# Moving the weight halves by 128 bytes in SBUF: two pad tiles of a two-layer hybrid-attention kernel resized

## The chip, the cores and the metric

The kernel runs on one NeuronCore of a Trainium2 chip. The metric is the device time of one execution in microseconds (us). TensorE multiplies matrices (the profile calls its matmuls PE and its weight loads PEld), VectorE is DVE, ScalarE is ACT, SyncE is SP and issues the transfers. SBUF is the on-chip memory: 128 partitions, and a tile takes the same byte range in each of them. What is changed here is where in that byte range the tiles stand.

## What is computed

Two layers act on one sequence of 256 tokens of width 1024, all in float32. A layer is a token mixer (sparse attention A with a top-64 selection, low-rank attention B, two gated branches, an output projection), a layer norm, a convolutional feed-forward network of inner width 2816, and a second layer norm. Shifts, scales and gates come from a conditioning vector `c`.

```python
def reference(x, c, ...):
    for l in range(DEPTH):                                   # DEPTH = 2
        mod = jax.nn.silu(c) @ w_ada[l] + b_ada[l]
        sh1, sc1, g1, sh2, sc2, g2 = jnp.split(mod[:, None, :], 6, axis=-1)
        h = x * (1.0 + sc1) + sh1
        y = token_mixer(h, positions, rel_bias, w_in[l], ...)
        x = layer_norm(DEEPNORM_ALPHA * x + g1 * y, ln1_g[l], ln1_b[l])
        h = x * (1.0 + sc2) + sh2
        y = conv_ffn(h, w_up[l], conv_w[l], conv_b[l], w_down[l])
        x = layer_norm(DEEPNORM_ALPHA * x + g2 * y, ln2_g[l], ln2_b[l])
    return x
```

## The kernel before

Activations stand with features on the partitions and the 256 tokens along the free dimension. All weights come as one long stream from HBM, in units of up to 2048 columns. `load` (from L192) issues each unit on the queue of SP into one of four `raw` tiles, as soon as the unit that had the tile is done with.

A float32 product is made of three faster ones. ACT rounds 1024 columns of a unit to the type float32r (`hi`, L245), DVE subtracts to get the rest (`lo`, L246); four tiles of each take turns. Activations are split in the same way into a tile with `hh` in its name and one with `hl` (`hhm`, `hlm` for the mixer, `hhf`, `hlf` for the feed-forward network, `h2h`, `h2l` for its inner activations, `nh`, `nl`, `ybh` and so on for smaller ones). `mm3` (L288) then issues hi·hh, hi·hl and lo·hh for each block of 128 output features: the weight block of 128 x 128 is loaded into TensorE as the stationary operand, 512 bytes a partition, and the activations are streamed past it as the moving operand, 256 columns or 1024 bytes a partition. Each matmul has its own weight load, so the two read SBUF at the same time, all through a stage. One stage has the roles the other way round: `main_va` (L610) loads blocks of `hhm` and `hlm` and streams `hi` and `lo`.

In the order of the program a layer is: `g1` (six banks of the input projection at once), `qa` and `va` with the index scores (`sc`, L549) between their matmuls, `uq`, `uk`, `uv`, the gates `ga` and `gb` with the attention's matmuls between them, the branches `wb` and `wa`, the output projection `wo`, then the feed-forward network: `up` (8 blocks together), 18 units `upp0` to `upp17` and the down projection `dn`. With 8 input blocks, 8 + 36 output blocks of `up` and `upp` and 22 x 8 of `dn`, and three passes each, that is 192 + 18 x 48 + 528 = 1584 matmuls a layer. In the names of the trace a digit for the layer and some buffer numbers are left in: `upp00b` is unit 0 of layer 0, `upp171b` unit 17 of layer 1, `b` the bank.

The places in SBUF follow from the order in which three pools are opened (`cp` for what lives throughout, `wp` for what streams through, `ap_` for activations) and from the sizes of the tiles. Two tiles that nothing uses, `wpad` and `apad` (L154, L155), move what comes behind them: `wpad` is the first tile of `wp`, `apad` of `ap_`.

Of the kernel before, what the change touches and what calls it, by code (L numbers as in the profile page):

```python
# [9 lines left out]
F32 = mybir.dt.float32  # L10
# [7 lines left out]
P = 128  # L18
# [121 lines left out]
def _build(nc, tc, ctx, stream, xt, cbc, ctr, posl, vecs, cst, outp, dbg=None):  # L140
    cp = ctx.enter_context(tc.tile_pool(name="cp", bufs=1))
    wp = ctx.enter_context(tc.tile_pool(name="wp", bufs=1))
    ap_ = ctx.enter_context(tc.tile_pool(name="ap", bufs=1))
# [7 lines left out]
        return pp.tile([P, 512], F32, name=name, tag=tag, bufs={"mm": 3, "at": 4, "st": 1}[tag])  # L151


    wp.tile([P, 24], F32, name="wpad", tag="wpad", bufs=1)  # L154
    ap_.tile([P, 232], F32, name="apad", tag="apad")  # L155


    pos_i = wp.tile([P, 64 + T], I32, name="pos_i", tag="cv", bufs=4)
# [992 lines left out]
```

## Time and profile before

| | |
|---|---|
| median of 3 runs | 818.27 us (816.04, 818.27, 823.65) |
| the profiled execution | 814.9 us, of which 813.1 us is the span that the trace covers |
| TensorE: matmuls, weight loads | busy 97% and 93% of the span, 6708 of each |
| VectorE, ScalarE | busy 84% and 63% |
| granted TensorE clock | 0.998 in the mean |
| transfers | 182 MB, 224 GB/s in the mean |

The profiled execution is 3.4 us under the median and 1.1 us under the fastest of the three runs. The span runs from the first to the last instruction; the 1.8 us beside it lie around it. Matmuls overlap in the pipeline, so the length that the trace gives for one (about 280 ns) is not what one costs: that is read from the distance of the starts, or from the chain of waits, which adds up what each stretch of matmuls took.

### The profile page before, as it was taken

To read this page: it belongs to the slowest core of one execution; us is meant where nothing else is said; L and a number is where in the kernel's file an instruction comes from. 1 tells how busy PE (TensorE), PEld (TensorE's weight loads), DVE (VectorE), ACT (ScalarE), POOL (GpSimd) and SP (SyncE) were. 2 spreads that over 40 slices of the span, in tenths; PEclk is the share of its full clock that TensorE was granted. 3 is DMA by queue.
4 is the path that set the end of the run, shared out by engine and by line. 5 is a ranking of instruction groups with operands and counts; after the bars stand their busy time and mean duration, and the time that the engine had idled before them with its cause. 6 is when DMAs were issued, how large, how long until landed. Compare 5 with 4: busy or idle time off the path is not lost.

```text
span 813.1 us, 16736 instructions
## 1 busy us (share of the span) xinstructions
PE 787.8 (97%) x6708; PEld 759.6 (93%) x6708; DVE 683.3 (84%) x1377; ACT 514.1 (63%) x898; POOL 0.2 (0%) x4
## 2 busy tenths in 40 slices
PE   5999999999999999999999998999999999999996
PEld 4898899989999999999999998998999999999995
DVE  6878798989997998899888898766899799897674
ACT  5987566564578766653547856647447976765452
POOL 0000000000000000000000000000000000000000
PEclk9999999999999999999999999999999999999999
DMA  8885758778655575579777856745564555565621
GB/s 295 319 327 204 233 176 310 292 268 304 223 192 183 183 256 166 184 260 328 294 253 240 295 178 233 260 174 189 216 206 163 203 199 194 184 242 195 213 73 52
DMA packets 29727, 182.07 MB, mean 224 GB/s; under 512 B 3857, under 2 KB 5841, under 8 KB 10578
## 3 DMA queue, kind: packets, MB, share of 16 engines
q1 hardware_dynamic: 29650, 181.01, 63.0%
q8 instruction: 52, 0.85, 0.4%
q14 instruction: 25, 0.20, 0.1%
HBM read 178.84 MB, written 1.05 MB: 221 GB/s over the span
## 4 chain that ended last, share of the span: by engine, by line
PE 73%; DVE 14%; DMA 5%; ACT 5%; issue 2%; SPq 0%; ACTq 0%; DVEq 0%
PE dn L290 15%; PE up L290 6%; DVE lo L246 5%; DMA raw<-stream 5%; DVE raw L231 2%; ACT hi L245 2%; PE wo L290 1%; PE g L290 1%; ACT step L378 1%; DMA pr<-misc 1%; PE adap L262 1%; PE bl L656 1%; PE gb11b L290 1%; PE gb10b L290 1%; PE qa00b L290 1%
## 5 line engine op out<-in xcount | busy, mean ns | idle before, releaser
L245 ACT ACTIVATE hi<-raw 128x1024 fp32r<-128x1024 f32 (+3 forms) x255 | 254.8, 1004 | 194.8 <-PE dn L290 48.1
L246 DVE TENSOR_TENSOR lo<-raw,hi 128x1024 fp32r<-128x1024 f32 (+3 forms) x255 | 293.1, 1154 | 73.8 <-ACT hi L245 72.6
L231 DVE SCALAR_TENSOR_TENSOR raw<-raw,cb 128x1024 f32<-128x1024 f32 x90 | 107.5, 1219 | 12.4 <-DMA raw<-stream 7.1
L290 PE MATMUL dn<-h2h,lo 128*128 128x256 f32 x352 | 98.3, 279 | 0.0
L290 PE MATMUL dn<-h2l,hi 128*128 128x256 f32 x352 | 98.3, 279 | 0.0
L290 PE MATMUL dn<-h2h,hi 128*128 128x256 f32 x352 | 98.1, 279 | 0.0
L290 PEld LDWEIGHTS dn<-h2h,lo 128*128 128x128 f32 x352 | 66.9, 190 | 0.1
L290 PEld LDWEIGHTS dn<-h2l,hi 128*128 128x128 f32 x352 | 66.1, 188 | 0.0
L290 PEld LDWEIGHTS dn<-h2h,hi 128*128 128x128 f32 x352 | 66.1, 188 | 0.0
L290 PE MATMUL g<-hhm,hi 128*128 128x256 f32 x168 | 45.6, 291 | 5.1 <-ACT hhm L1020 5.0
L290 PE MATMUL g<-hhm,lo 128*128 128x256 f32 x168 | 44.5, 286 | 0.0
L290 PE MATMUL g<-hlm,hi 128*128 128x256 f32 x168 | 42.5, 280 | 0.0
L290 PEld LDWEIGHTS g<-hhm,hi 128*128 128x128 f32 x168 | 32.0, 195 | 7.3 <-ACT hhm L1020 6.8
L675 ACT ACTIVATE pr<-pr,mx 128x128 f32<-128x128 f32 x64 | 28.4, 446 | 12.3 <-DVE mx L672 12.3
L290 PE MATMUL up<-hhf,lo 128*128 128x256 f32 x128 | 34.8, 279 | 0.0
L290 PE MATMUL up<-hhf,hi 128*128 128x256 f32 x128 | 34.6, 280 | 0.0
L290 PE MATMUL up<-hlf,hi 128*128 128x256 f32 x128 | 33.2, 280 | 0.0
L290 PEld LDWEIGHTS g<-hhm,lo 128*128 128x128 f32 x168 | 31.8, 196 | 0.2 <-DVE lo L246 0.2
L290 PEld LDWEIGHTS g<-hlm,hi 128*128 128x128 f32 x168 | 30.3, 188 | 0.1
L290 PEld LDWEIGHTS up<-hhf,lo 128*128 128x128 f32 x128 | 24.3, 190 | 0.0
L290 PEld LDWEIGHTS up<-hhf,hi 128*128 128x128 f32 x128 | 23.8, 188 | 0.5 <-DVE hhf L973 0.5
L378 ACT ACTIVATE step<-posf,thr 128x256 bf16<-128x256 f32 (+1 forms) x64 | 23.2, 443 | 1.4 <-DVE thr L346 1.4
(904 smaller groups left out, 2665.5 us busy)
## 6 DMA issues: line engine op xcount, KB each, us to landing
raw<-stream SPq DMA_DIRECT2D x149, 1024.0 KB, 4.9
raw<-stream SPq DMA_DIRECT2D x21, 768.0 KB, 4.9
raw<-stream SPq DMA_DIRECT2D x5, 512.0 KB, 4.4
raw<-stream SPq DMA_DIRECT2D x4, 384.0 KB, 3.5
kT<-rl SPq DMA_DIRECT2D x8, 128.0 KB, 4.3
XB<-xt SPq DMA_DIRECT2D x3, 256.0 KB, 8.1
out<-XA SPq DMA_DIRECT2D x3, 256.0 KB, 2.5
XB<-xt SPq DMA_DIRECT2D x2, 128.0 KB, 6.4
```

The source lines that it names most:

```text
L231: V.scalar_tensor_tensor(out=raw[:, c:c + D], in0=raw[:, c:c + D], scalar=1.0, in1=cb, op0=OP.mult, op1=OP.mult, accum_out=mod[l][:, j:j + 1])
L245: S.activation(hi[:, a:e], raw[:, c + a:c + e], AF.Copy)
L246: x = V.tensor_sub(lo[:, a:e], raw[:, c + a:c + e], hi[:, a:e].bitcast(F32))
L262: PE.matmul(b[:, :T], ct[:, k:k + 1].to_broadcast([P, P]), raw[:, k * T:(k + 1) * T], start=(k == 0), stop=(k == KD - 1))
L290: PE.matmul(out, whl[p // 2][:, wcol], xhl[p % 2][xsl], start=start and p == 0, stop=stop and p == 2, skip_group_check=True)
L378: S.activation(st, posf[:, 64 + (0 if g < 32 else P):], AF.Sign, bias=thr[:, g:g + 1])
L656: PE.matmul(bs[e][:, P:384], q[:, P:T], k, start=False, stop=True, skip_group_check=True)
L675: S.activation(p[:, sl], p[:, sl], AF.Exp, bias=mx[:, j:j + 1], scale=-1.0, accum_out=ssum[:, h, j:j + 1])
```

## The change

`wpad` grows from 24 to 56 columns, 128 bytes, and `apad` shrinks from 232 to 200, the same 128 bytes. So all of `wp` moves up by 128 bytes, and the rest stays. The order of the instructions on each engine, and what each one works on, is the same row by row.

```diff
-    wp.tile([P, 24], F32, name="wpad", tag="wpad", bufs=1)
-    ap_.tile([P, 232], F32, name="apad", tag="apad")
+    wp.tile([P, 56], F32, name="wpad", tag="wpad", bufs=1)
+    ap_.tile([P, 200], F32, name="apad", tag="apad")
```

The byte at which the tiles start in a partition, modulo 256, as the built programs have it:

| tiles | before | after |
|---|---|---|
| `hi`, `lo` (all 8 tiles; every weight block in them is a multiple of 512 bytes further) | 0 | 128 |
| `raw`, `cv`, `pr`, `rl`, `rsA`, `mt` (the few small tiles of `wp` move by the same 128) | 0 | 128 |
| `hh..`, `hl..`, `h2h`, `h2l`, `nh`, `nl`, `ybh`, `yah`, `gate` and all else of `ap_` | 192 | 192 |
| `XA`, `XB`, `cb` (of `cp`) | 0 | 0 |
| the part of `vec` that is loaded with 470 columns | 64 | 64 |

For the pair of addresses that TensorE reads at once, moving minus stationary modulo 256, this gives:

| stage | before | after |
|---|---|---|
| all stages through `mm3` (weights stationary) | 192 - 0 = 192 | 192 - 128 = 64 |
| `va` (activations stationary) | 0 - 192 = 64 | 128 - 192 = 192 |

## Rows read from the trace of the kernel before

**Rows 1.** The page: busy time of each engine, share of the span, instructions.

```profile
PE 787.8 (97%) x6708; PEld 759.6 (93%) x6708; DVE 683.3 (84%) x1377; ACT 514.1 (63%) x898; POOL 0.2 (0%) x4
```

**Rows 2.** The page: chain that ended last, shares of the span by engine.

```profile
PE 73%; DVE 14%; DMA 5%; ACT 5%; issue 2%; SPq 0%; ACTq 0%; DVEq 0%
```

**Rows 3.** The same chain in order of time, layer 0: start us, us, what, matmuls.

```profile
105.85 5.65 PE ga00b L290 x48
...
213.34 5.44 PE wo20b L290 x48
...
230.26 22.73 PE up L290 x192
253.00 5.65 PE upp00b L290 x48
...
349.11 5.65 PE upp170b L290 x48
...
372.88 44.65 PE dn L290 x379
```

**Rows 4.** The same chain, layer 1, and one of its transfers.

```profile
440.39 7.37 DMA raw<-stream
...
496.82 5.47 PE ga01b L290 x48
...
620.33 22.12 PE up L290 x192
642.45 5.44 PE upp01b L290 x48
...
734.93 5.44 PE upp171b L290 x48
...
757.41 43.65 PE dn L290 x385
```

**Rows 5.** Windows, TensorE alone: stretch, us, busy (x), granted clock, DMA share, GB/s.

```profile
253.00:355.00 102.00, 102.00 (x868) 1.00 0.57 196
642.40:745.00 102.60, 102.60 (x908) 1.00 0.58 203
```

**Rows 6.** Timeline, layer 1, qa behind sc: start us, length, engine, line, out<-moving,stationary.

```profile
466.57 0.39 PE L290 MATMUL qa11b<-hhm,hi 128*128 128x256 f32 x1
466.79 0.28 PE L290 MATMUL qa11b<-hlm,hi 128*128 128x256 f32 x1
...
467.14 0.28 PE L290 MATMUL qa11b<-hlm,hi 128*128 128x256 f32 x1
...
469.18 0.28 PE L290 MATMUL qa11b<-hlm,hi 128*128 128x256 f32 x1
```

**Rows 7.** The same timeline, layer 1, va behind sc.

```profile
474.14 0.39 PE L610 MATMUL va<-hi,hhm 128*128 128x256 f32 x1
474.37 0.28 PE L610 MATMUL va<-lo,hhm 128*128 128x256 f32 x1
...
474.60 0.28 PE L610 MATMUL va<-hi,hhm 128*128 128x256 f32 x1
...
484.02 0.28 PE L610 MATMUL va<-hi,hlm 128*128 128x256 f32 x1
```

**Rows 8.** Groups by line and shape: busy us, mean ns, idle before.

```profile
L246 DVE TENSOR_TENSOR lo<-raw,hi 128x512 fp32r<-128x512 f32 x16 | 11.0, 688 | 1.3 <-ACT hi L245 1.1
L764 DVE TENSOR_TENSOR hlg<-gate,hhg 128x512 fp32r<-128x512 f32 x8 | 5.2, 688 | 0.0
...
L824 ACT ACTIVATE h2h<-sq 128x256 fp32r<-128x256 f32 x44 | 17.8, 405 | 4.5 <-DVE sq L822 4.4
L1027 ACT ACTIVATE XA<-XB 128x256 f32<-128x256 f32 x8 | 2.8, 406 | 1.3 <-DMA XB<-xt 1.3
```

**Rows 9.** Transfers: out<-in, count, KB of one, us from issue to landing.

```profile
raw<-stream SPq DMA_DIRECT2D x1, 256.0 KB, 5.6
...
vec<-vecs SPq DMA_DIRECT2D x1, 235.0 KB, 5.0
```

## The prediction, made before the changed kernel was run

> **What bounds the kernel now.** I read the page first, for the engine that is busy, then the chain of waits in order of time, for what a matmul costs in each stage, then the timeline around pauses, and last the groups and transfers for what else touches the moved tiles. TensorE is busy 97% of the span, and its weight loads 93% [rows 1]: a load runs beside nearly every matmul. Of the chain that ended last, 73% is TensorE, 14% VectorE and 5% transfers [rows 2]. So the kernel is bound by the pace of its matmuls, above all in the two feed-forward networks, where the chain is TensorE without a break.
>
> That pace has two values. In layer 0 a unit of 48 matmuls of `upp` takes 5.65 us, the first as the last of 18, which is 117.7 ns a matmul; in layer 1 the same unit takes 5.44 us, 113.3 ns, again from the first to the last [rows 3, 4]. `up` takes 22.73 us and 22.12 us for 192 matmuls. A part of `dn` takes 44.65 us for 379 in layer 0, 117.8 ns, and 43.65 us for 385 in layer 1, 113.4 ns. The granted clock is 1.00 in both layers, over 102 us each, and so are the transfers much alike, a share of 0.57 and 0.58 [rows 5]; neither makes the difference. I call the two paces fast (113.3) and slow (117.8); the step between them is 4.4 ns a matmul.
>
> It is not the places alone either. `wo` and `upp` of layer 0 read the same `hi`, `lo` and `hh` tiles in the same way, and `wo20b` takes 5.44 us for its 48 where `upp00b` takes 5.65 [rows 3]. The gate `ga`, with the same tiles in both layers, takes 5.65 us in layer 0 and 5.47 in layer 1 [rows 3, 4]. So with weights at 0 and streams at 192 both paces exist, and a stretch keeps the one in which it has settled: 18 units of `upp` in a row.
>
> What a stretch settles at behind a pause is where the place shows. In layer 1 `qa` and `va` are interrupted by the same index scores. Behind them `qa` starts at 466.57 us, the second matmul follows after 0.22 us, and from 467.14 to 469.18 us there are 18 steps, 113.3 ns each: fast [rows 6]. `va` starts at 474.14 us, the second matmul follows after 0.23 us, and from 474.60 to 484.02 us there are 80 steps, 117.8 ns each: slow [rows 7]. `va` has the roles exchanged: its moving operand minus its stationary one is 64 modulo 256, where it is 192 in `qa`. That 64 is what the change gives to every stage but `va`.
>
> **The change part by part.** It removes and adds no instruction, and no wait; order and queues are the same. Four things read or write what moves.
>
> First, TensorE. If the pair's difference decides where a stretch settles, all stages through `mm3` now settle as `va` did, slow. The change in time is then counted in matmuls on the chain that were fast before, by 4.4 ns each. The feed-forward network of layer 1 has 1584 of them: 1584 x 4.44 ns = 7.0 us. Checked against the rows: `up` 22.73 - 22.12 = 0.6 us, 18 x (5.65 - 5.44) = 3.8 us, and 528 x 4.4 ns = 2.3 us for `dn`, together 6.7 us; I take 7.0. `ga` of layer 1 has three whole units at the fast pace, 3 x 0.18 = 0.5 us, and the last three units of `wo` have 144 matmuls in each layer, 288 x 4.44 ns = 1.3 us [rows 3, 4]. That makes 8.8 us. What is slow already, the feed-forward network of layer 0 and its `ga`, stays. `va` itself would turn fast, about 200 matmuls or 0.9 us, but there the chain goes through `lo`, so I count nothing back. In the other direction, if everything settled fast, the network of layer 0 gives back 7.0 us and its `ga` 3 x 0.21 = 0.6 us, 7.6 us in all; and with the short slow stretches between the attention's matmuls, which I leave uncounted, perhaps 1 us more (a guess).
>
> Second, ACT and DVE, which write `hi` and `lo` and read `raw`. I cost this at nothing. The subtraction of 512 columns takes 688 ns on tiles at 0 (`lo`) and 688 ns on tiles at 192 (`hlg`); the copy of 256 columns takes 406 ns on tiles at 0 (`XA`) and 405 ns into a tile at 192 (`h2h`) [rows 8]. Were it not nothing, DVE would be hurt first, being busy 84%, and `lo` would come late in the stages where the chain goes through it, 14% of the span.
>
> Third, the transfers into `raw`, whose lines of 8 KB a partition now start at 128. A transfer to `vec` at 64 modulo 256 landed after 5.0 us for 235 KB, one to `raw` at 0 after 5.6 us for 256 KB, 21 and 22 ns a KB [rows 9]: no loss shows. Transfers are 5% of the chain, about 40 us, one of the pieces 7.37 us long [rows 2, 4]. I take nothing; the upper bound is the spread of those two rows, 3% of 40 us, 1.2 us, and a gain I exclude, since no row has a line shortened by its place.
>
> The Trainium skill speaks against the change here. "DMA: Bandwidth & Descriptors", section "How a descriptor splits into AXI transactions", says that a transaction starts at a multiple of 256 bytes, so that a line which doesn't start at one needs an extra partial transaction. As an estimate from that page, a line of 8 KB goes from 256 beats to 260, 1.6%, which on 40 us of the chain is 0.6 us; no run here has `raw` elsewhere than at 0.
>
> Fourth, `cv`, `pr` and `rl`, which the attention's matmuls read: the matmuls there pause for other engines, and their rows are not counted.
>
> **The sum.** Against the profiled execution's 814.9 us: 814.9 + 8.8 = 823.7 us. The median of the runs is 818.27, 3.4 us above it, and their spread, 816.04 to 823.65, is 7.6 us, about what one feed-forward network at the other pace is worth (7.0). I read that as runs in which other stretches settled slow; it is not shown by these rows. 823.7 is 0.7% above the median, within the 1% that a measurement of this kernel can tell from no change.
>
> **Rivals.** *The place decides nothing* and each stretch settles by the accident of its pause, as `upp` did differently in the two layers. For it: the same tiles ran at both paces [rows 3, 4]. Against it: `qa` and `va` behind the same scores. The time is then that of before, 814 to 824, in the middle 818.3. "TensorE: Matmul & The Clock Gate", Part 2 of the Trainium skill, in the step on LDWEIGHTS, says that TensorE has two independent SBUF read ports, so that loading the next weights takes nothing from the running matmul. By that rule this rival is the case; the trace neither shows nor excludes it, since the cause of the 4.4 ns is not in any row.
>
> *Settling fast.* The difference of 64 may favour the fast pace behind other pauses than the scores; `up` and `dn` start behind quite different matmuls, and `va` shows one kind of pause only. Against it: the 80 slow steps of `va`. Then 814.9 - 7.6 = 807.3 us, down to 806 with the short stretches. It is faster by more than 1% below 810.1 us.
>
> *A third pace, slower still.* A weight block of 512 bytes at 128 covers parts of three stretches of 256 bytes, where it covered two. Were each weight load in `mm3` to lose another step of 4.4 ns, the 3168 matmuls of the two feed-forward networks alone would add 3168 x 4.44 = 14.1 us to 823.7: 837.8 us. Against it: the blocks of `hhm` that `va` loads start at 192, cover three as well, and went at 117.8 and no slower. It decides from a pace of 118.6 ns: 826.5 us, 1% over the median, is 2.8 us above 823.7, and 2.8 us / 3168 = 0.9 ns.
>
> **How the numbers follow.** Slow nearly everywhere, 823.7 us, its own range 820 to 827: 0.45, since `qa` and `va` are the only rows that differ in the pair alone, but are few. The place decides nothing, 818.3: 0.27. Fast, 807.3: 0.18. A third pace or a cost on other engines, over 827: 0.10. The range for 8 in 10 leaves out the lower half of the fast case and the upper cases: 807 to 828. Faster by over 1% (under 810.1): most of the fast case, 0.17. Slower by over 1% (over 826.5): the last case and a third of the first one, where the short stretches come on top of 823.7: 0.25. Within 1%: 0.58.
>
> **What would show it.** Right: in the chain of waits both layers' `upp` units at 5.65 us, `wo` too, and the matmuls of `va` at 113 ns. Wrong: `upp` at 5.44 in both layers (fast), one of each as now (nothing decided), or any unit of 48 over 5.75 (a third pace). The row of `lo` should keep 688 ns for 512 columns, and `raw` should land in the same time; a longer mean there would make the second or third cost wrong.

## The result and the profile after

The changed kernel takes 827.64 us in the median of 11 runs (825.97 to 831.51), the kernel before in the same session 818.27 us (815.15 to 823.65, also 11). The ratio is 1.0113 with a 95% interval of 1.0085 to 1.014: slower by a bit over 1%. Where a ratio is given here, runs more than 1.5% above the fastest of their kernel are left out of it as slow, so it can differ from the ratio of the two medians, which are over all runs. The forecast was 823.7 us, a loss of 0.7%, in a range of 807 to 828, and 0.25 was its chance for a loss of over 1%. The profiled execution took 826.4 us, its span is 824.6 us, 11.5 us longer than before.

The page of after, busy time of each engine: TensorE's matmuls are 11.1 us longer busy and its weight loads 11.9, the other engines as before to 2 us, beside [rows 1].

```profile
PE 798.9 (97%) x6708; PEld 771.5 (94%) x6708; DVE 685.2 (83%) x1377; ACT 513.6 (62%) x898; POOL 0.2 (0%) x4
```

The chain of waits of after, in order of time (start us, us, what, matmuls), with the places of [rows 3, 4]:

```profile
106.50 5.65 PE ga00b L290 x48
...
214.55 5.65 PE wo20b L290 x48
...
231.90 22.73 PE up L290 x192
254.63 5.65 PE upp00b L290 x48
...
350.74 5.65 PE upp170b L290 x48
...
374.51 44.65 PE dn L290 x379
...
499.86 5.65 PE ga01b L290 x48
...
625.15 22.73 PE up L290 x192
647.88 5.65 PE upp01b L290 x48
...
743.99 5.65 PE upp171b L290 x48
...
767.21 45.34 PE dn L290 x385
```

Every whole unit of 48 on the chain is at 5.65 or 5.66 us now, 117.7 ns a matmul, where before `wo20b`, `upp01b` to `upp171b` and (nearly) `ga01b` were at 5.44. `dn` of layer 1 takes 45.34 us for its 385 matmuls, 117.8 ns, where it took 43.65. What was slow before has not changed by a hundredth: `up` of layer 0 takes 22.73 us, a part of its `dn` 44.65 us. On the chain there is no pace beyond the two.

The timeline of after behind the index scores, layer 1, `qa` first and then `va` (start us, length, engine, line, out<-moving,stationary), against [rows 6, 7]:

```profile
473.08 0.39 PE L290 MATMUL qa11b<-hhm,hi 128*128 128x256 f32 x1
473.30 0.28 PE L290 MATMUL qa11b<-hlm,hi 128*128 128x256 f32 x1
...
473.54 0.28 PE L290 MATMUL qa11b<-hhm,hi 128*128 128x256 f32 x1
...
474.48 0.28 PE L290 MATMUL qa11b<-hhm,lo 128*128 128x256 f32 x1
...
476.92 0.39 PE L610 MATMUL va<-hi,hhm 128*128 128x256 f32 x1
477.14 0.28 PE L610 MATMUL va<-lo,hhm 128*128 128x256 f32 x1
...
477.37 0.28 PE L610 MATMUL va<-hi,hhm 128*128 128x256 f32 x1
...
479.98 0.28 PE L610 MATMUL va<-hi,hlm 128*128 128x256 f32 x1
```

The two have exchanged their paces. `qa` goes from 473.54 to 474.48 us in 8 steps, 117.5 ns each: slow, where it was fast. `va` goes from 477.37 to 479.98 us in 23 steps, 113.5 ns each: fast, where it was slow.

### The profile page after: what moved, and what is told of

It is laid out like the page before. It is cut to its first block, busy times and chain, and to the rows that moved or that the text cites. A ratio compares the mean times of both kernels' runs of the same rounds, so it can differ in the third digit from the quotient of the medians.

```text
span 824.6 us, 16736 instructions
## 1 busy us (share of the span) xinstructions
PE 798.9 (97%) x6708; PEld 771.5 (94%) x6708; DVE 685.2 (83%) x1377; ACT 513.6 (62%) x898; POOL 0.2 (0%) x4
## 4 chain that ended last, share of the span: by engine, by line
PE 75%; DVE 11%; DMA 6%; ACT 5%; issue 2%; SPq 0%; ACTq 0%; DVEq 0%
PE dn L290 15%; PE up L290 6%; DMA raw<-stream 5%; DVE lo L246 4%; DVE raw L231 2%; ACT hi L245 1%; PE wo L290 1%; PE g L290 1%; ACT step L378 1%; DMA pr<-misc 1%; PE adap L262 1%; PE bl L656 1%; PE wo01b L290 1%; PE wo00b L290 1%; PE qa00b L290 1%
## 5 line engine op out<-in xcount | busy, mean ns | idle before, releaser
L290 PE MATMUL dn<-h2h,lo 128*128 128x256 f32 x352 | 98.6, 280 | 0.0
L290 PE MATMUL dn<-h2l,hi 128*128 128x256 f32 x352 | 98.5, 280 | 0.0
L290 PE MATMUL dn<-h2h,hi 128*128 128x256 f32 x352 | 98.2, 279 | 0.0
L290 PEld LDWEIGHTS dn<-h2l,hi 128*128 128x128 f32 x352 | 66.1, 188 | 0.0
L290 PEld LDWEIGHTS dn<-h2h,lo 128*128 128x128 f32 x352 | 66.0, 187 | 0.1
L290 PEld LDWEIGHTS dn<-h2h,hi 128*128 128x128 f32 x352 | 66.0, 187 | 0.0
L290 PE MATMUL g<-hhm,hi 128*128 128x256 f32 x168 | 46.0, 293 | 5.1 <-ACT hhm L1020 5.1
L290 PE MATMUL g<-hhm,lo 128*128 128x256 f32 x168 | 44.7, 287 | 0.0
L290 PE MATMUL g<-hlm,hi 128*128 128x256 f32 x168 | 43.0, 282 | 0.0
L290 PEld LDWEIGHTS g<-hhm,hi 128*128 128x128 f32 x168 | 31.9, 195 | 7.3 <-ACT hhm L1020 6.8
L675 ACT ACTIVATE pr<-pr,mx 128x128 f32<-128x128 f32 x64 | 28.4, 447 | 11.9 <-DVE mx L672 11.9
L290 PE MATMUL up<-hhf,lo 128*128 128x256 f32 x128 | 35.0, 280 | 0.0
L290 PE MATMUL up<-hhf,hi 128*128 128x256 f32 x128 | 34.7, 281 | 0.0
L290 PE MATMUL up<-hlf,hi 128*128 128x256 f32 x128 | 33.2, 279 | 0.0
L290 PEld LDWEIGHTS g<-hhm,lo 128*128 128x128 f32 x168 | 31.7, 195 | 0.0
L290 PEld LDWEIGHTS g<-hlm,hi 128*128 128x128 f32 x168 | 30.2, 187 | 0.1
L290 PEld LDWEIGHTS up<-hhf,hi 128*128 128x128 f32 x128 | 23.7, 187 | 0.5 <-DVE hhf L973 0.5
L290 PEld LDWEIGHTS up<-hhf,lo 128*128 128x128 f32 x128 | 24.0, 188 | 0.0
```

The source lines that it names most:

```text
L290: PE.matmul(out, whl[p // 2][:, wcol], xhl[p % 2][xsl], start=start and p == 0, stop=stop and p == 2, skip_group_check=True)
L675: S.activation(p[:, sl], p[:, sl], AF.Exp, bias=mx[:, j:j + 1], scale=-1.0, accum_out=ssum[:, h, j:j + 1])
```

## The experiments

The theory, "pair", is that the difference of the two places that TensorE reads at once, moving minus stationary modulo 256, decides at which pace a stretch settles. All these kernels compute the same with the same instructions; only pads differ. Ratios are to the kernel before, run on the same chip in the same session; the diffs are against it too. Where a pad adds lines to the kernel, L290 is L292 or L294 in its trace.

### Which places matter

Both places 128 bytes further (`wpad` as in the change, `apad` left at 232):

```diff
-    wp.tile([P, 24], F32, name="wpad", tag="wpad", bufs=1)
+    wp.tile([P, 56], F32, name="wpad", tag="wpad", bufs=1)
```

> Weight halves at 128 and streamed tiles at 64, both 128 bytes further than in the kernel before, so that moving minus stationary is 192 again. Theory 'pair' (the difference modulo 256 decides at which pace a stretch settles): as the kernel before, about 818 us, most stretches at 113.3 ns a matmul, va at 117.8. Rival 'absolute' (a weight block that starts at 128 is slow to load, wherever the streams stand): as the changed kernel, about 827 us, upp at 5.65 us for 48 in both layers.

Measured: 816.29 us, ratio 0.9936 (0.9897 to 0.9974). Weight blocks that start at 128 are no slower to load; "absolute" falls. That it came out 0.6% faster, where "pair" has it the same, is not explained. The chain of waits of this run shows the two paces again:

```profile
252.54 5.44 PE upp00b L290 x48
...
345.02 5.44 PE upp170b L290 x48
...
637.65 5.65 PE upp01b L290 x48
...
733.76 5.65 PE upp171b L290 x48
```

Here layer 0 is the fast one and layer 1 the slow one, the other way round than in [rows 3, 4]. With a difference of 192 it is open at each start of a feed-forward network which pace it gets.

The streams moved instead of the weights (`wpad` 24 as before, `apad` 200):

> Weight halves and all else of their pool at 0 as before, streamed tiles at 64 instead of 192, so that moving minus stationary is 64. 'Pair': as the changed kernel, about 827 us, upp at 5.65 us for 48 in both layers, va at 113.3 ns. 'Absolute': as the kernel before, about 818 us.

Measured: 827.06 us, ratio 1.0097 (1.0062 to 1.0132). Not one tile of `wp` has moved, and the loss is the whole of that of the change. Its chain of waits:

```profile
254.37 5.65 PE upp00b L290 x48
...
649.07 5.65 PE upp01b L290 x48
```

The tiles around the weights moved, the weight halves not:

```diff
-    wp.tile([P, 24], F32, name="wpad", tag="wpad", bufs=1)
-    ap_.tile([P, 232], F32, name="apad", tag="apad")
+    wp.tile([P, 56], F32, name="wpad", tag="wpad", bufs=1)
+    ap_.tile([P, 168], F32, name="apad", tag="apad")
...
+            if not split:
+                wp.tile([P, 32], F32, name="hpad", tag="hpad", bufs=1)
             hi = wp.tile([P, 1024], F32R, name=f"hi{i}", tag="whi", bufs=NHI)
```

> raw, cv, pr and rl at 128, weight halves put back to 0 by a second pad ahead of them, streams at 192. 'Pair': as the kernel before, about 818 us. Rival 'others' (the transfers into raw, or what ACT and DVE read and write there, carry the loss): as the changed kernel, about 827 us, with lo, hi or the landing of raw longer.

Measured: 820.18 us beside 820.25, ratio 0.9957 (0.9918 to 0.9996). Nothing is lost by `raw`, `cv`, `pr` and `rl` at 128, the transfers into them included; "others" falls. This rests on the times: the one traced execution is the longest of the ten (829.43 us, granted clock 0.987 in the mean and 1.00 over `up` and `upp`) and has `upp` at 5.65 us in both layers, so at 192 both networks can be slow too.

The weight halves and the few small tiles behind them moved (`wpad` 24, the same `hpad`, `apad` 200):

> Only the weight halves (and the small tiles behind them) at 128; raw, cv, pr and rl stay at 0, streams at 192. 'Pair' and 'absolute': as the changed kernel, about 827 us. 'Others': as the kernel before, about 818 us.

Measured: 826.94 us, ratio 1.0094 (1.0057 to 1.0132), the loss of the change. Its chain of waits has both feed-forward networks slow, but a unit between them fast:

```profile
254.37 5.65 PE upp00b L292 x48
...
579.57 5.45 PE wb11b L292 x48
...
648.27 5.65 PE upp01b L292 x48
```

That `wb11b`, and the matmuls of `wa` behind it, went at 113.3 ns at a difference of 64. So 64 makes the slow pace far more likely and does not force it.

So the times of the four runs divide as "pair" says and as neither "absolute" nor "others" does: 192 gives the time of before (e1, e3), 64 gives that of after (e2, e4).

### Other differences

Weights at 0, streams at 128, at 0, at 160, at 224 (`apad` 216, 248, 224, 240):

> Weight halves at 0, streamed tiles at 128: moving minus stationary 128, halfway between the kernel before (192) and the changed one (64). Theory 'nearness' (the share of stretches that settle slow changes step by step with the difference): between the two, 820 to 825 us. Rival 'two kinds' (a difference is either of the kind of 192 or of the kind of 64): 818 or 827 us. va has minus 128, which is the same 128: if the pair is all that counts, va settles like the rest.

> Weight halves and streamed tiles both at 0: moving minus stationary 0, for va too. 'Nearness': 0 is as far from 192 as from 64, so 820 to 825 us. If equal places collide in every matmul, a third pace: every 1 ns a matmul above 117.8 is 4 us or more above 827.

> Weight halves at 0, streamed tiles at 160. 'Nearness': a bit above the kernel before, 819 to 823 us. If all stretches could settle fast at some difference, the time is about 807 us: 814.9 less 7.6 us, as worked out ahead.

> Weight halves at 0, streamed tiles at 224. 'Nearness': 816 to 823 us, on the far side of 192 from 64. If all stretches settle fast, about 807 us.

| difference | time us | ratio, interval |
|---|---|---|
| 128 | 832.54 | 1.012 (1.0055 to 1.0186) |
| 0 | 836.68 | 1.017 (1.0103 to 1.0236) |
| 160 | 828.57 | 1.008 (1.0048 to 1.0111) |
| 224 | 831.71 | 1.0122 (1.0084 to 1.016) |

"Nearness" and "two kinds" both fall: 128 lies outside of 192 and 64, and both neighbours of 192 are slower than it. There are more than two paces. The chains of waits, a unit of `upp` in each layer, for 128:

```profile
256.10 5.69 PE upp00b L290 x48
...
652.93 5.70 PE upp01b L290 x48
```

for 0:

```profile
257.60 5.76 PE upp00b L290 x48
...
655.73 5.76 PE upp01b L290 x48
```

and for 160:

```profile
254.91 5.70 PE upp00b L290 x48
...
648.97 5.63 PE upp01b L290 x48
```

That is 118.6, 120.0 and 117.3 to 118.8 ns a matmul; for 224 it is 5.68 us, 118.3 ns. At 0, equal places, the step over the fast pace is 6.7 ns. `va`, which has 128 as well in the run at 128, goes like the rest there: 80 steps from 481.87 to 491.36 us, 118.6 ns each. Of the six differences tried, 192 is the only one at which a unit of `upp` was seen at 5.44 us. So the kernel before stood at the best of the six, with one of its two networks slow by what looks like accident.

Modulo 256 or modulo more? The streams 256 bytes further (`apad` 296):

> Streamed tiles 256 bytes further than in the kernel before, weight halves at 0: the same 192 modulo 256, but 192 instead of 448 modulo 512. If the places count modulo 256: as the kernel before, 818 to 821 us, stretches at both paces. If they count modulo 512 or more: another share of slow stretches, 827 us where nearly all are.

Measured: 817.15 us, ratio 1.0005 (0.9963 to 1.0047), and both paces again in the chain of waits:

```profile
256.83 5.44 PE upp00b L290 x48
...
643.31 5.65 PE upp01b L290 x48
```

So nothing asks for a period beyond 256, though one run at another 256 does not prove it, and a period of 128 could not tell 192 from 64.

### hi and lo at places of their own

A weight load runs beside the matmul before its own. The timeline of the kernel before shows which:

```profile
300.30 0.28 PE L290 MATMUL upp80b<-hlf,hi 128*128 128x256 f32 x1
300.30 0.19 PEld L290 LDWEIGHTS upp80b<-hhf,lo 128*128 128x128 f32 x1
```

The load of `lo` starts with the matmul that streams `hlf`, to the hundredth of a us. So `hl` meets `lo`, and `hh` meets `hi`. A pad between the two tags gives these pairs differences of their own:

```diff
+            if not split:
+                wp.tile([P, 32], F32, name="lpad", tag="lpad", bufs=1)
             lo = wp.tile([P, 1024], F32R, name=f"lo{i}", tag="wlo", bufs=NLO)
```

Only `lo` at 128 (`wpad` 24, `apad` 200):

> Only lo at 128; hi at 0, streams at 192. While a matmul streams hl, the weight load beside it is of lo; while one streams hh, it is of hi. So the pair is 64 beside every third matmul (hl and lo) and 192 beside the other two. Theory 'each pair its own share': two thirds like the kernel before, about 821 us. Rival 'one bad pair sets the stretch': slow all over, about 827 us. If the mixture breaks the slow pattern: about 807 us.

Measured: 812.24 us beside 816.62, ratio 0.994 (0.9909 to 0.9971). That is no further below the kernel before than e1 was, so the time alone would not show that the pad helps; the chain of waits does:

```profile
252.11 5.44 PE upp00b L292 x48
...
344.59 5.44 PE upp170b L292 x48
...
372.86 7.46 DMA raw<-stream
...
383.88 9.96 DMA raw<-stream
...
639.58 5.44 PE upp01b L292 x48
...
732.06 5.44 PE upp171b L292 x48
```

Both layers are fast now. The gain is 4.4 us by the medians, 2.9 by the traced executions (812.03 against 814.9), and not the 7.6 worked out ahead. The two transfers say where a part went: in `dn` of layer 0 the chain now waits for `raw`, which it did not in the kernel before. The windows of `dn` of layer 0 up to the first matmul of the next layer (stretch, us, then busy us of PE, PEld, DVE, ACT, POOL with their counts, granted clock, DMA share, GB/s) show it, for this kernel

```profile
350.03:420.05 70.02, 66.15 (x556) 64.44 (x554) 60.15 (x102) 31.62 (x42) 0.00 (x0) 1.00 0.82 290
```

for the kernel before

```profile
354.76:422.69 67.93, 67.93 (x555) 66.67 (x554) 60.57 (x101) 31.66 (x42) 0.00 (x0) 1.00 0.81 296
```

and for e1, whose layer 0 is as fast:

```profile
350.46:416.78 66.32, 65.87 (x555) 64.37 (x554) 60.48 (x102) 31.86 (x42) 0.00 (x0) 1.00 0.85 308
```

The kernel with `lo` at 128 is at `dn` 4.7 us earlier than the one before, and 2.6 us earlier through it: TensorE has 1.8 us less to do there, but stands still for 3.9 of 70.0 us, where it never did. So 2.1 us of the lead are gone. It is not the price of fast matmuls as such: e1 reaches `dn` as early and stands still for under half a us. Why the transfers were later in the one than in the other is open.

Only `hi` at 128, `lo` at 0 (`hpad` and `lpad` of 32 columns, `apad` 168):

> Only hi at 128; lo at 0, streams at 192. The pair is 64 beside two matmuls of three (hh and hi) and 192 beside the third (hl and lo). 'Each pair its own share': about 824 us. 'One bad pair sets the stretch': about 827 us. If the mixture breaks the slow pattern: about 807 us.

Measured: 821.35 us beside 816.62, ratio 1.0027 (0.9983 to 1.0071), between the theories. Its chain of waits has `upp` fast in both layers, but a pace of `dn` that neither kernel has, 45.17 us for 380 matmuls, 118.9 ns:

```profile
346.84 5.44 PE upp170b L294 x48
...
370.36 45.17 PE dn L294 x380
```

Only `lo` at 64 (`lpad` of 16 columns, `apad` 216):

> Only lo moved, to 64 instead of the 128 of the run e9: the pair is 128 beside every third matmul (hl and lo), 192 beside the other two. At 128 all through (run e5) no stretch was fast. Theory 'unequal pairs break the slow pattern', whatever the odd one is: as e9, about 812 us, ratio 0.994 to the kernel before. Rival 'each pair its own share': a third of the way from the kernel before to e5, ratio 1.004, about 822 us. Rival 'one bad pair sets the stretch': as e5, ratio 1.012.

Measured: 829.79 us, ratio 1.0163 (1.012 to 1.0206), with both layers at 118.1 to 118.3 ns:

```profile
259.61 5.67 PE upp00b L292 x48
...
654.17 5.68 PE upp01b L292 x48
```

An unequal third does not by itself give the fast pace that e9 had, so that theory falls; "one bad pair sets the stretch" fits this run, but not e9, whose odd pair of 64 is the one that is slow throughout in e2. Why 64 helps beside `lo` and hurts beside all is open, and so is how the two reads hinder each other: no row shows a conflict, only the time between starts.

## Why the prediction was right, and where it was short

**The bound.** That the kernel is bound by the pace of its matmuls, and that it has two paces at the same clock, came out so: the span grew by 11.5 us and TensorE's busy time by 11.1.

**The mechanism.** That the difference of the pair weighs on where stretches settle, read from `qa` and `va` alone, held for every whole unit on the chain; the change made the rest of the kernel into what `va` was, and `va` into what `qa` was. The runs e1 to e4 show it apart from all else that moved. But it is a matter of odds and not the rule as it was put. Counted by the starts in the timelines, over stretches of ten steps or more without a pause, 44 of 59 were fast (under 115.5 ns in the mean) at 192 in the kernel before, and still 7 of 58 at 64 in the changed one. So two rows of one pause each could have misled; that they did not was in part luck. That `va` is fast after was said ahead, and could have been the first sign against it.

**The sum.** It was 2.7 us short: 823.7 against 826.4 for the profiled execution. By the starts on the chain, before and after:

| stretch | before | after | difference | forecast |
|---|---|---|---|---|
| network of layer 1, `up` to the end of `dn` | 180.73 | 187.40 | +6.67 | +7.0 |
| `ga` of layer 1 up to the last unit | 16.34 | 16.96 | +0.62 | +0.5 |
| `wb`, `wa`, `wo` of both layers, from the second half of `wb00b` and from `wb11b` on up to `up` | 94.24 | 95.99 | +1.75 | +1.3 (`wo` alone) |
| from the end of layer 0 to `ga` of layer 1 | 79.29 | 80.70 | +1.41 | 0 |
| from the start to the second half of `wb00b` | 181.37 | 182.31 | +0.94 | 0 |
| network of layer 0 | 187.27 | 187.26 | 0 | 0 |
| what is left | 73.9 | 74.0 | +0.1 | 0 |

The terms that were worked out came within 0.5 us; for the network the check by the rows, 6.7, was nearer than the 7.0 that was taken. What the sum lacked lies in the two stretches put at nothing, 2.35 us, and most of that is not matmuls. The same six transfers are on the chain in them in both kernels, and in e2 too, where `raw` and `pr` stand at 0 as before (us of each, in order of time):

| | first `raw` | `raw` ahead of `wb` of layer 0 | three of `raw` behind layer 0 | `pr` behind them | sum |
|---|---|---|---|---|---|
| before | 6.25 | 6.43 | 7.00, 5.73, 7.37 | 6.91 | 39.69 |
| after | 6.69 | 6.57 | 7.17, 6.37, 7.39 | 7.45 | 41.64 |
| e2 | 6.72 | 6.16 | 7.68, 6.41, 7.84 | 7.62 | 42.43 |

So 1.95 of the 2.35 us are transfers that took longer on the chain. They took longer still in e2, so the place of `raw` does not explain it; whether it comes with slower matmuls or by chance stays open, with one trace of each kernel. The other 0.4 us are left for the short stretches of matmuls there, and as much came from `wb` and `wa` beside `wo` in the table, near the "perhaps 1 us" that the forecast named for the gain and left out of the loss.

**The place of the median.** 823.7 was set beside the median of 818.27 although it was made against an execution of 814.9, 3.4 us faster than that; what the sum adds belongs on the median as well in so far as its runs had fast stretches left. So the measured 827.64 lies above the 820 to 827 that the forecast gave to its own case, and the loss of 1.1% in the part to which it gave a quarter: the range held by 0.4 us, while every sign named for the mechanism came. The other half of that step, that runs of before differ by which stretches settle slow, got support: 31 runs of before in one session lie between 811.8 and 825.7 us, 18 of them with a granted clock of 0.997 or more still between 811.8 and 824.9, while the 10 runs of e4, at a difference of 64, lie between 824.7 and 830.2, nine of them with that clock between 824.7 and 827.9. And e1 shows the layers with their paces exchanged. A kernel that is slow nearly throughout varied less than one that is slow by accident.

**What was costed at nothing.** ACT and DVE kept their times, and so did the transfers of 1024 KB by their median. The groups of after:

```profile
L246 DVE TENSOR_TENSOR lo<-raw,hi 128x512 fp32r<-128x512 f32 x16 | 11.0, 688 | 1.7 <-ACT hi L245 1.4
```

and its transfers:

```profile
raw<-stream SPq DMA_DIRECT2D x149, 1024.0 KB, 4.9
```

688 ns for `lo` at 128 as at 0 [rows 8]; the page's row of before for these 149 transfers of 1024 KB had 4.9 us too. The extra transaction of the Trainium skill ("DMA: Bandwidth & Descriptors", "How a descriptor splits into AXI transactions") would have been 0.6 us, as an estimate by its figures, too little for these runs to see. The run e3, which moves `raw` and leaves the halves, shows no loss.

**The rivals.** "The place decides nothing" is out by e2 and e4. By "TensorE: Matmul & The Clock Gate", Part 2 of the Trainium skill, loading the next weights takes no read bandwidth of SBUF from the matmul that runs. The measurement speaks against it for this kind of stream, float32r weights of 512 bytes beside 1024 bytes of moving columns: moving the streams alone by 128 bytes costs 1% (e2), moving both costs nothing (e1), and putting both at the same place costs 1.7% (e6). "A third pace" did not come with the change, but it exists, at the differences of 128 and 0, and with `lo` at 64. "Settling fast" did not come either, but for the kernel of e9, with 64 in the pair of `hl` and `lo` alone.

## What to carry to other kernels

Where TensorE is the bound and one matmul after another brings its own weight load, read the time between starts in long stretches: if the same instructions go at two paces at a full clock, look at where the two operands stand modulo 256 bytes, and try pads, for the stationary halves apart too. Judge such a change by many runs and by the chain of waits of each, since a stretch that settles by accident moves a run by 7 us here. And when matmuls get faster, look at what they then wait for: of 4.7 us won before `dn` of layer 0 in e9, 2.1 were lost again to waits for transfers, though in e1 hardly any were. Set the transfers on the chain beside each other as well, before a difference between two traces is put down to the change.

## What the runs showed of the hardware that was not expected

- The start of an operand in SBUF, modulo 256 bytes, changes the pace of float32r matmuls of 256 columns with a weight load each: 113.3, 117.3 to 118.9 and 120.0 ns in the long stretches, all at a granted clock of 1.00 there.
- It is the difference that counts, as far as tried: weights at 128 and streams at 64 gave 0.9936 of the time of 0 and 192 (a gain that is not explained, where a loss of 1% was in question), streams 256 further gave 1.0005.
- At a difference of 192 two paces are stable, and a stretch keeps the one that it has got, over 18 units of 48 matmuls; the units of `upp` in layers 0 and 1 were slow and fast in the kernel before, fast and slow in e1 and e11, and slow in both in e3.
- A slow stretch can turn fast without a pause when the pair changes: in the timeline of after, `qa` is slow up to 474.48 us and `va` right behind it, from 474.72 to 475.85 us, has 10 steps of 113 ns. And the fast pace can go on at 64 when it is entered without a pause: `uq`, behind `va` in the same trace, has 35 steps of 113.4 ns.

```profile
486.55 0.28 PE L290 MATMUL uq<-nh,hi 128*128 128x256 f32 x1
...
490.52 0.28 PE L290 MATMUL uq<-nh,lo 128*128 128x256 f32 x1
```
